# Feed-forward of a two-layer encoder: one weight group's casts held behind the last bank reads, and a spare tile for two of the seven down products

## The chip, the cores and the metric

The kernel runs on one core of a Trainium2 chip. The metric is the device time of one execution in microseconds (us). The core has a matrix engine (PE in the profile; PEld is its weight load), a vector engine (DVE), a scalar engine (ACT), a slower elementwise engine (POOL) and a sync engine (SP), whose queue issues nearly all transfers between HBM and the on-chip memory (SPq are its issues). Matrix products accumulate in eight banks, and DVE or ACT read them out. About 0.2% of the time (4.2 us) is the smallest difference that a measurement of this kernel tells from no change.

## The reference, cut to what matters

Two layers over 1024 tokens of width 1024. Each layer has a token mixer, a cross-attention to 256 memory tokens, an output projection, and then the feed-forward that this change touches:

```python
h = rmsnorm(x, norm_ffn[i])
gu = h @ w_gate_up[i]                                  # 1024 -> 2 * 2816
x = x + (jax.nn.silu(gu[..., :D_FF]) * gu[..., D_FF:]) @ w_down[i]   # 2816 -> 1024
```

All data are float32. After the second layer a final norm gives the output.

## The kernel before

Every product is made with operands that are split in two: `hi` (line 106, an ACT cast to the matrix engine's type) gives the rounded value, and `lo` (line 109, a DVE subtraction; its instruction stands at line 110 in the profile) gives the rest. Each product then takes three matmuls (high by high, high by low, low by high). A tile named `wd` holds the split weights of the down projection, a tile `hB` the split right operand.

The feed-forward multiplies by a seven-product scheme in place of eight products of half blocks (a Strassen form with few sums). It has two stages.

**Gate and up.** Units `Pair` (lines 1043 and on) make pairs of 128 output rows; 22 pairs, taken two at a time. For each two pairs the seventh products are made together by a unit `Fourth`, in three steps A, B and C. The matmuls of `Pair.product` stand at line 1101, those of `Fourth.part` at line 1183. A method `read` takes each finished bank out: ACT copies at lines 1112 to 1126 (the copy of product 4's bank X into `c` is line 1126), DVE additions through the helper at line 1109, and DVE subtractions through the helper at line 1211. The last steps of the stage, counted backwards as `to_go`, are: -6 the second pair's product 3, -5 step A, -4 its product 4, -3 step B, -2 its product 5, -1 step C. In step A bank Y is written in its low half, and `sub(a.c1[:, low], Y[:, low])` reads it; step B writes the high half of the same bank.

**Down.** Eleven row blocks are done as six groups `g` of two (the last has one). The products are numbered `i` in the code and go in the order 0, 1, 3, 2, 4, 5, 6; each has 132 matmuls (line 1532), 24 for a group of two. Products 0, 2 and 4 sum up in the four banks X, products 1 and then 3 and 5 in the four banks Y. After a product's last group `read(i, ...)` (the addition at line 1496) takes the banks out; product 3 begins Y anew, so it must wait for the reads of product 1, and product 4 goes on in X, so it waits for the reads of product 2.

`left_side(i, g)` (line 1406) makes the left operand of product `i`, group `g`. Raw weights come by transfer into a ring of five tiles `wd_raw` (`raw_tile`, 512 KB each) or into six tiles `wd_kept`. Product 0 uses a half `a` of `wd_kept`; product 3 loads two raw tiles and adds them into the other half `b` (line 1429); product 2 uses `b - a` (line 1423); product 4 loads two raw tiles and subtracts one from the other (line 1435); product 5 loads one and subtracts (line 1439). The result is cast into a ring of three tiles `wd`. `right_side(i, g)` reloads the right operand from HBM (`b_raw`) and casts it into `hB`.

`left_side` is called two groups ahead of use. For product 0 the calls stand inside the gate and up stage, by the table `ahead`: `left_side` of group 0 at `to_go` -5, of group 1 at -3. A scheduler in the framework sets the final order of each engine's queue: it takes instructions by priority as it expects their operands to be ready, so that the order is not the order of the code. Every queue is then run strictly in that order.

Of the kernel before, what the change touches and what calls it, by code (L numbers as in the profile page):

```python
# [41 lines left out]
def trunk_kernel(ctx: ExitStack, tc: tile.TileContext, a: dict, out: bass.AP):  # L42
# [59 lines left out]
    def raw_tile(name):  # L102

        return phase[0].tile([P, D], F32, tag="raw", name=name, bufs=phase[2])

    def hi(dst, src):
        nc.scalar.copy(dst, src)  # L107

    def lo(dst, src, h, eng=None):
        (eng or nc.vector).tensor_tensor(dst, src, h.bitcast(F32), op=ALU.subtract)  # L110

    def load_w(src, tag="whl", bufs=3, eng=None, name="w", pool=wp, parts=1, raw=None):
        if raw is None:
# [72 lines left out]
    class Norm:  # L186
# [82 lines left out]
        def raw(self, which):  # L269

            bc = self.scale()
            for k in range(NK):
                nc.vector.scalar_tensor_tensor(
                    self.xs[k], self.xs[k], gains[:, which, k : k + 1], bc, op0=ALU.mult, op1=ALU.mult
                )
                yield k
# [265 lines left out]
    for layer in range(2):  # L542
# [467 lines left out]
        with (  # L1010
# [32 lines left out]
            class Pair:  # L1043
# [62 lines left out]
                def read(self, n):  # L1106
                    self.seen.add(n)
                    X, Y = self.X, getattr(self, "Y", None)
                    add = lambda o, p_, q_, op=ALU.add: nc.vector.tensor_tensor(o, p_, q_, op=op)
                    if n == 0:  # L1110
                        self.g1 = temp("g1")
                        nc.scalar.copy(self.g1, X)
                    elif n == 1:
                        add(self.g1, Y, self.g1)
                        nc.scalar.activation(self.g1, self.g1, AF.Silu)
                    elif n == 2:
                        self.g2 = temp("g2")
                        nc.scalar.copy(self.g2, X)
                    elif n == 3:
                        self.c2 = temp("c2")  # L1120
                        nc.scalar.copy(self.c2, Y)  # L1121
                        if 4 in self.seen:
                            add(self.c2, self.c2, self.c1)
                    elif n == 4:
                        self.c1 = temp("c1")
                        nc.scalar.copy(self.c1, X)
                        if 3 in self.seen:
                            add(self.c2, self.c2, self.c1)
                        if 5 in self.seen:
                            add(self.c2, self.c2, self.g2, ALU.mult)  # L1130
                    elif n == 5:
                        add(self.g2, Y, self.g2)
                        nc.scalar.activation(self.g2, self.g2, AF.Silu)
                        if 4 in self.seen:
                            add(self.c2, self.c2, self.g2, ALU.mult)
                    else:
                        add(self.c1, self.c1, X, ALU.subtract)
                        add(self.c1, self.c1, self.g1, ALU.mult)
# [3 lines left out]
            class Fourth:  # L1142
# [65 lines left out]
                def read(self, n):  # L1208
                    (a, b), X, Y = self.units, self.X, self.Y
                    low, high = slice(0, h2), slice(h2, HS)  # L1210
                    sub = lambda c, ps, op=ALU.subtract: nc.vector.tensor_tensor(c, c, ps, op=op)
                    if n == "A":
                        sub(a.c1[:, low], X[:, low])
                        sub(a.c1[:, low], Y[:, low])
                    elif n == "B":
                        sub(a.c1[:, high], X[:, low])
                        sub(b.c1[:, high], Y[:, high])
                    else:
                        sub(
                            b.c1.rearrange("p (n c) -> p n c", n=2),  # L1220
                            X[:, low].unsqueeze(1).to_broadcast([P, 2, h2]),
                        )
                        sub(b.c1[:, low], X[:, high], ALU.add)
                        sub(b.c1, b.g1, ALU.mult)
                        sub(a.c1[:, high], Y[:, high])
                        sub(a.c1, a.g1, ALU.mult)
# [166 lines left out]
            def two(t, n):  # L1393
                return t.rearrange("p (n c) -> p n c", c=HS)[:, :n]
# [5 lines left out]
            def keep_rows(g):  # L1400
                if g not in kept:
                    p, n = groups[g]
                    kept[g] = fp.tile([P, 2, 2, HS], F32, tag="t8", name="wd_kept", bufs=6)[:, :n]
                    rows(kept[g][:, :, 0], g, 0, slice(0, HS))

            def left_side(i, g):

                p, n = groups[g]
                first_cols, second_cols = slice(0, HS), slice(HS, D)

                def raw():
                    return raw_tile("wd_raw").rearrange("p (n c) -> p n c", c=HS)[:, :n]

                if i == 0:
                    keep_rows(g)
                a, b = kept[g][:, :, 0], kept[g][:, :, 1]
                if i == 0:
                    src = a
                elif i == 1:
                    src = raw()  # L1420
                    rows(src, g, 1, first_cols)
                elif i == 2:
                    nc.vector.tensor_tensor(a, b, a, op=ALU.subtract)
                    src = a
                elif i == 3:
                    r, o = raw(), raw()
                    rows(r, g, 0, second_cols)
                    rows(o, g, 1, second_cols)
                    nc.vector.tensor_tensor(b, r, o, op=ALU.add)
                    src = b  # L1430
                elif i == 4:
                    src, o = raw(), raw()
                    rows(src, g, 0, first_cols)
                    rows(o, g, 0, second_cols)
                    nc.vector.tensor_tensor(src, src, o, op=ALU.subtract)
                elif i == 5:
                    src = raw()
                    rows(src, g, 1, first_cols)
                    nc.vector.tensor_tensor(src, src, a, op=ALU.subtract)
                else:  # L1440
                    src = raw()
                    rows(src, g, 1, second_cols)
                w = wp.tile([P, 2, D], F32R, tag="whl", name="wd", bufs=3)
                hi(two(w[:, 0], n), src)
                lo(two(w[:, 1], n), src, two(w[:, 0], n))
                for q in range(n):
                    left[i, p + q] = w[:, :, q * HS : (q + 1) * HS]

# [145 lines left out]
            }  # L1594
            for to_go in gate_up():
                for what, g in ahead.get(to_go, ()):
                    what(g) if what is keep_rows else what(0, g)
            norms = [Norm(row=None if is_a else next(factor_rows)), Norm()]
            ends = {c: Norm(HS // 2, 7) for c in quarter}
            dorder = [(i, g) for i in (0, 1, 3, 2, 4, 5, 6) for g in range(len(groups))]  # L1600
# [136 lines left out]
```

## Time and profile before

| what | value |
|---|---|
| three runs | 2115.09, 2116.83, 2116.86 us (median 2116.83) |
| the profiled execution's own time | 2115.94 us |
| its span, first to last instruction | 2114.2 us (so 1.74 us lie around it) |
| mean granted PE clock | 0.998 |
| PE, DVE, ACT, POOL busy | 99%, 72%, 51%, 28% of the span |
| HBM traffic | 133 GB/s over the span |

The first layer's feed-forward passes from gate and up to down at 814.45 us, the second layer's at 1888.38 us. A row of the timeline gives the start, the length from the first start to the last end of a merged run of equal instructions, engine, line, operation, output and inputs, shapes, count, and in square brackets the engine's idle time before it and what ended that. The end of a matmul is modelled by the profile; its start is recorded.

### The profile page before, as it was taken

What the parts mean: (1) busy time and instruction counts of PE and PEld (TensorE: products, weight loads), DVE (VectorE), ACT (ScalarE), POOL (GpSimd) and SP (SyncE); (2) the same over time, 40 slices, a digit from 0 to 9 for tenths busy, and PEclk for the clock granted to TensorE, in tenths of its full rate; (3) what the DMA queues carried; (4) which work ended last, traced back from release to release, by engine and by line L of the source; (5) the groups of instructions that cost most, each with busy time, mean ns of one, the idle gap of its engine ahead of it and who ended that gap; (6) DMA issues with size and microseconds to landing.
All of it is one profiled execution on the core that took longest, in us unless ns stands there. A gap on an engine that the chain in (4) does not pass through costs nothing.

```text
span 2114.2 us, 29053 instructions
## 1 busy us (share of the span) xinstructions
PE 2092.7 (99%) x10318; PEld 1750.1 (83%) x10318; DVE 1524.6 (72%) x2474; ACT 1077.9 (51%) x2037; POOL 583.6 (28%) x615
## 2 busy tenths in 40 slices
PE   9999999999999999999999999999999999999998
PEld 8788888888888888888888888888888888888887
DVE  7687886987666667776766666677986666677675
ACT  6687775544434335344466666664543434344443
POOL 0344330334444430000233223203243444400001
PEclk9999999999999999999999999999999999999999
DMA  6421128332333227866232222275232333267662
GB/s 232 146 82 51 36 83 288 99 115 100 110 108 111 91 105 254 313 216 207 78 110 68 69 72 78 64 266 157 75 110 105 110 115 104 91 254 256 205 221 95
DMA packets 121778, 288.08 MB, mean 136 GB/s; under 512 B 12705, under 2 KB 21153, under 8 KB 121633
## 3 DMA queue, kind: packets, MB, share of 16 engines
q1 hardware_dynamic: 113744, 272.42, 38.4%
q10 hardware_dynamic: 7888, 13.79, 1.7%
q8 instruction: 82, 1.34, 0.3%
q14 instruction: 64, 0.52, 0.1%
HBM read 211.19 MB, written 68.95 MB: 133 GB/s over the span
## 4 chain that ended last, share of the span: by engine, by line
PE 80%; issue 12%; DVE 3%; ACT 2%; POOL 2%; DMA 1%; POOLq 0%; ACTq 0%; SPq 0%; DVEq 0%
PE X L1101 16%; PE Y L1101 16%; PE mm L141 15%; PE po L141 8%; PE X L1532 5%; PE Y L1532 4%; PE O L809 3%; PE S L746 3%; PE pT L789 3%; PE X L1183 2%; PE Y L1183 2%; PE mm L448 1%; ACT p L761 1%; POOL wS L1058 1%; POOL wf L110 1%
## 5 line engine op out<-in xcount | busy, mean ns | idle before, releaser
L1101 PE MATMUL Y<-hB,wgu 128*128 128x512 f32 x1056 | 255.5, 391 | 0.8 <-ACT c L1121 0.8
L1101 PE MATMUL X<-hB,wgu 128*128 128x512 f32 x1056 | 254.8, 391 | 0.0
L1532 PE MATMUL X<-hB,wd 128*128 128x512 f32 (+1 forms) x1092 | 243.2, 383 | 0.9 <-DVE x L1496 0.9
L110 DVE TENSOR_TENSOR wgu<-wS,wgu 128x1024 fp32r<-128x1024 f32 (+1 forms) x124 | 155.4, 1253 | 120.9 <-ACT wgu L107 120.7
L1532 PEld LDWEIGHTS X<-hB,wd 128*128 128x128 f32 x1092 | 200.2, 188 | 41.4 <-issue 1.7
L1101 PEld LDWEIGHTS Y<-hB,wgu 128*128 128x128 f32 x1056 | 196.8, 188 | 43.4 <-ACT c L1121 1.6
L1101 PEld LDWEIGHTS X<-hB,wgu 128*128 128x128 f32 x1056 | 196.0, 188 | 39.8
L774 POOL TENSOR_SCALAR p<-p,stat 128x384 f32<-128x384 f32 (+1 forms) x256 | 143.1, 579 | 308.7 <-DVE stat L771 213.4
L141 PE MATMUL mm<-hT,wqk 128*128 128x512 f32 x672 | 199.3, 405 | 0.0
L107 ACT CAST wgu<-wS 128x1024 fp32r<-128x1024 f32 (+1 forms) x124 | 114.3, 923 | 142.0 <-POOL wS L1058 124.6
L141 PE MATMUL po<-yT,wo 128*128 128x512 f32 x768 | 184.2, 393 | 0.0
L1532 PE MATMUL Y<-hB,wd 128*128 128x512 f32 x792 | 180.4, 389 | 0.0
L1532 PEld LDWEIGHTS Y<-hB,wd 128*128 128x128 f32 x792 | 148.6, 188 | 31.2 <-DVE x L1496 0.4
L244 POOL TENSOR_TENSOR nr<-nv,neg_half 128x4 f32<-128x4 f32 (+1 forms) x12 | 13.3, 1105 | 582.9 <-DVE nv L243 573.7
L141 PEld LDWEIGHTS po<-yT,wo 128*128 128x128 f32 x768 | 142.7, 188 | 28.8 <-DVE yT L110 0.2
L1101 PE MATMUL X<-hT,wgu 128*128 128x512 f32 x624 | 150.2, 391 | 0.0
L107 ACT CAST hB<-b_raw 128x512 fp32r<-128x512 f32 x154 | 89.4, 618 | 115.5 <-DMA b_raw<-b_d 100.3
L1058 POOL TENSOR_TENSOR wS<-wgu_raw 128x512 f32<-128x512 f32 x44 | 61.2, 1391 | 292.1 <-DVE wgu L110 292.1
L1101 PEld LDWEIGHTS X<-hT,wgu 128*128 128x128 f32 x624 | 116.8, 188 | 26.3
L761 ACT ACTIVATE p<-p,stat 128x256 f32<-128x256 f32 (+1 forms) x192 | 112.4, 587 | 48.1 <-DVE stat L757 46.0
L110 DVE TENSOR_TENSOR pl<-pT,ph 128x384 fp32r<-128x384 f32 (+1 forms) x256 | 119.0, 493 | 19.1 <-ACT ph L107 15.9
L110 DVE TENSOR_TENSOR hB<-b_raw,hB 128x512 fp32r<-128x512 f32 x154 | 99.9, 687 | 42.2 <-ACT hB L107 42.1
(201 smaller groups left out, 4248.1 us busy)
## 6 DMA issues: line engine op xcount, KB each, us to landing
wgu_raw<-in_w_gu SPq DMA_DIRECT2D x92, 512.0 KB, 3.7
wd_raw<-in_w_dn SPq DMA_DIRECT2D x70, 512.0 KB, 4.4
b_raw<-b_d SPq DMA_DIRECT2D x70, 512.0 KB, 5.4
b_d<-c SPq DMA_DIRECT2D x88, 256.0 KB, 2.1
b_d<-t SPq DMA_DIRECT2D x66, 256.0 KB, 2.2
wo_raw<-in_w_out SPq DMA_DIRECT2D x32, 512.0 KB, 3.5
xr_d<-x ACTq DMA_DIRECT2D x32, 256.0 KB, 2.5
xr<-xr_d SPq DMA_DIRECT2D x16, 512.0 KB, 6.1
```

The costliest lines, as they stand in the source:

```text
L107: nc.scalar.copy(dst, src)
L110: (eng or nc.vector).tensor_tensor(dst, src, h.bitcast(F32), op=ALU.subtract)
L141: nc.tensor.matmul(ps[:, :n], l, r, start=start and i == 0 and j == 0, stop=stop and i == len(order) - 1 and j == 2,)
L746: nc.tensor.matmul(s_[:, :n], Q[self.h][:, qb * P : (qb + 1) * P], k, start=j == 0, stop=j == 1)
L761: nc.scalar.activation(p[:, :n], p[:, :n], AF.Exp, bias=m1, scale=-1.0, accum_out=s1)
L774: nc.gpsimd.tensor_scalar(p[:, :n], p[:, :n], ri[:, i : i + 1], 1.0, op0=ALU.mult, op1=ALU.mult)
L789: nc.tensor.transpose(tr[:, j * P : (j + 1) * P], p[:, j * P : (j + 1) * P], ident)
L809: nc.tensor.matmul(o[:, c0 : c0 + w * P], self.value(j), t[:, s0 : s0 + w].rearrange("p j q -> p (j q)"), start=j == js[0] and t is self.p ...
L1058: sub = lambda o, p_, q_: nc.gpsimd.tensor_tensor(o, p_, q_, op=ALU.subtract)
L1101: nc.tensor.matmul(ps, l, r, start=n in (0, 1, 3, 6) and k == 0 and i == 0, stop=k == 3 and i == 2, skip_group_check=True,)
L1183: nc.tensor.matmul(bank[:, at : at + h2], l, r, start=start and k == 0 and i == 0, stop=stop and k == 1 and i == 2, skip_group_check=True,)
L1532: nc.tensor.matmul(bank[:, c], l, r, start=i in (0, 1, 3, 6) and p == 0 and n == 0, stop=p == HF - 1 and n == 2, skip_group_check=True,)
```

## The change

First, `read` keeps two instructions of the last two pairs: the ACT copy of bank X of product 4 (`copied`) and the DVE subtraction that reads bank Y in step B (`summed`). The casts of `left_side(0, 1)`, group 1 of the down projection's product 0, get an ordering edge: the `hi` cast stands behind `copied` on ACT and the `lo` subtraction behind `summed` on DVE. The edge orders the queue of one engine and adds no semaphore wait.

Second, after the gate and up stage a tile `wd_other` of 128 x 2 x 1024 is taken from the pool slot `w8`, which the stage used for a weight tile (`wgu2`). Its two halves, by the parity of `g`, take the second raw operand of products 3 and 4, which used to come from the ring of five `wd_raw`. (In the short title of the change these are the fourth and fifth by number.)

```diff
-                        nc.scalar.copy(self.c1, X)
+                        self.copied = nc.scalar.copy(self.c1, X)
...
-                        sub(b.c1[:, high], Y[:, high])
+                        b.summed = sub(b.c1[:, high], Y[:, high])
...
-            def left_side(i, g):
+            def left_side(i, g, behind=()):
...
+                def other():
+                    t = spare[g % 2].bitcast(F32)
+                    return t.rearrange("p (n c) -> p n c", c=HS)[:, :n]
...
                 elif i == 3:
-                    r, o = raw(), raw()
+                    r, o = raw(), other()
...
                 elif i == 4:
-                    src, o = raw(), raw()
+                    src, o = raw(), other()
...
-                hi(two(w[:, 0], n), src)
-                lo(two(w[:, 1], n), src, two(w[:, 0], n))
+                with ExitStack() as queued:
+                    for ins in behind:
+                        queued.enter_context(tc.issue_after(ins.ins))
+                    hi(two(w[:, 0], n), src)
+                    lo(two(w[:, 1], n), src, two(w[:, 0], n))
...
-                    what(g) if what is keep_rows else what(0, g)
+                    if what is keep_rows:
+                        keep_rows(g)
+                    elif what is left_side:
+                        left_side(0, g, (us[-1].copied, us[-1].summed) if g == 1 else ())
+                    else:
+                        what(0, g)
+            spare = fp.tile([P, 2, D], F32R, tag="w8", name="wd_other", bufs=1)
+            spare = spare[:, 0], spare[:, 1]
```

The queues of PE and POOL keep their order. No instruction is added or left out on any engine; DVE, ACT and SP change their order in the stretch from step A to the end of the down projection, in both layers alike but for a few rows. Three places show it; the first layer's rows stand for both.

The first place is the end of gate and up on DVE. `wd<-wd_kept,wd` are the `lo` subtractions of the down groups, `c<-c,X` and `c<-c,Y` the reads of the banks of steps A and B. Before (-) and now (+):

```order
 L110 TENSOR_TENSOR wd<-wd_kept,wd 128x1024
 L1211 TENSOR_TENSOR c_7626<-c_7626,X_7746 128x256
-L110 TENSOR_TENSOR wd<-wd_kept,wd 128x1024
 L1211 TENSOR_TENSOR c_7626<-c_7626,Y_7747 128x256
 L1109 TENSOR_TENSOR c_7742<-c_7742,c_7777 128x512
 L1211 TENSOR_TENSOR c_7626<-c_7626,X_7746 128x256
 L1211 TENSOR_TENSOR c_7777<-c_7777,Y_7747 128x256
+L110 TENSOR_TENSOR wd<-wd_kept,wd 128x1024
```

Group 1's subtraction has moved from ahead of the read of bank Y to behind all four reads of steps A and B.

The second place is DVE ahead of the reads of product 1 (`x<-Y`), which free the banks Y for product 3. Before:

```order
L1429 TENSOR_TENSOR wd_kept<-wd_raw 128x2x512
L110 TENSOR_TENSOR wd<-wd_kept,wd 128x1024
L110 TENSOR_TENSOR hB<-b_raw,hB 128x512 x2
L1423 TENSOR_TENSOR wd_kept<-wd_kept 128x2x512
L1429 TENSOR_TENSOR wd_kept<-wd_raw 128x2x512
L1496 TENSOR_TENSOR x_01_8057<-Y,x_01_8057 128x512
L110 TENSOR_TENSOR wd<-wd_kept,wd 128x1024
```

Now, with the addition at line 1433, the subtraction `b - a` at line 1427 and the read at line 1503:

```order
L1433 TENSOR_TENSOR wd_kept<-wd_raw,wd_other 128x2x512
L110 TENSOR_TENSOR wd<-wd_kept,wd 128x1024
L110 TENSOR_TENSOR hB<-b_raw,hB 128x512 x2
L1433 TENSOR_TENSOR wd_kept<-wd_raw,wd_other 128x512
L1427 TENSOR_TENSOR wd_kept<-wd_kept 128x2x512
L1427 TENSOR_TENSOR wd_kept<-wd_kept 128x512
L1503 TENSOR_TENSOR x_01_8058<-Y,x_01_8058 128x512
L110 TENSOR_TENSOR wd<-wd_kept,wd 128x1024
```

The last addition of product 3 (the 128x512 one) and the last two subtractions of product 2 have moved ahead of the read; they stood behind it.

The third place is DVE ahead of the reads of product 2 (`x<-X`), which free the banks X for product 4. Before:

```order
L110 TENSOR_TENSOR wd<-wd_raw,wd 128x1024
L110 TENSOR_TENSOR hB<-b_raw,hB 128x512 x2
L1435 TENSOR_TENSOR wd_raw<-wd_raw 128x1024
L110 TENSOR_TENSOR wd<-wd_raw,wd 128x1024
L1496 TENSOR_TENSOR x_00_8736<-X,xr 128x512
L1496 TENSOR_TENSOR x_10_8741<-X,xr 128x512
```

Now:

```order
L110 TENSOR_TENSOR wd<-wd_raw,wd 128x1024
L110 TENSOR_TENSOR hB<-b_raw,hB 128x512 x2
L1503 TENSOR_TENSOR x_00_8729<-X,xr 128x512
L110 TENSOR_TENSOR wd<-wd_raw,wd 128x1024
L1503 TENSOR_TENSOR x_10_8734<-X,xr 128x512
```

Product 4's fifth subtraction (`wd_raw<-wd_raw` of 128x1024) has left the place ahead of the read; it now stands before the reads of product 3. In the second layer it stood behind these reads already, and there the sixth one (128x512) has come to stand directly ahead of the first `x<-X`.

On SP the first two `wd_other` transfers now go out behind the first reload `b_raw` of product 1, ahead of the other five.

More of the change, by code (lines that the diff above doesn't have):

```diff
@@ L106, in hi @@
     def hi(dst, src):
-        nc.scalar.copy(dst, src)
+        return nc.scalar.copy(dst, src)
     def lo(dst, src, h, eng=None):
-        (eng or nc.vector).tensor_tensor(dst, src, h.bitcast(F32), op=ALU.subtract)
+        return (eng or nc.vector).tensor_tensor(dst, src, h.bitcast(F32), op=ALU.subtract)
     def load_w(src, tag="whl", bufs=3, eng=None, name="w", pool=wp, parts=1, raw=None):
```

## The prediction

> **What bounds the kernel now.** I read the page's busy shares, then what PE waits for, then the timeline of PE through the two feed-forward stages, then DVE, ACT and SP at the places where PE stopped.
>
> ```profile
> span 2114.2 us, 29053 instructions
> PE 2092.7 (99%) x10318; PEld 1750.1 (83%) x10318; DVE 1524.6 (72%) x2474; ACT 1077.9 (51%) x2037; POOL 583.6 (28%) x615
> PE bc L266 <- DVE diag L252: 1.8, 2, 1.6
> PE Y L1183 <- DVE c L1211: 1.5, 1, 1.5
> PE X L1532 <- DVE x L1496: 0.9, 1, 0.9
> ```
>
> PE is busy 2092.7 of 2114.2 us, and its work is not changed. So the change can only win back time in which PE stands still. The waits list two such places inside the touched stretch, one each in line 1183 (gate and up) and line 1532 (down), 1.5 and 0.9 us. The other large one, 1.6 us of line 266, is in the kernel's tail. This caps the gain near 3 us, or 0.14%: less than the 0.2% that a measurement can tell. What is open is whether the new order of DVE makes other stops.
>
> **Term 1: the last steps of gate and up.** Second layer's PE rows, then the first layer's:
>
> ```profile
> 1880.27 0.88 PE L1183 MATMUL X<-q4h,wgu 128*128 128x256 f32 x6
> 1882.67 0.97 PE L1183 MATMUL Y<-hT,wgu 128*128 128x256 f32 x6 [1.53 <-DVE c L1211]
> 1883.48 2.90 PE L1101 MATMUL Y<-hB,wgu 128*128 128x512 f32 x12
> 1886.22 1.60 PE L1183 MATMUL X<-q4h,wgu 128*128 128x256 f32 x12
> 1887.66 0.88 PE L1183 MATMUL Y<-hT,wgu 128*128 128x256 f32 x6
> ...
> 808.04 0.88 PE L1183 MATMUL X<-q4h,wgu 128*128 128x256 f32 x6
> 809.54 2.91 PE L1101 MATMUL Y<-hB,wgu 128*128 128x512 f32 x12
> ```
>
> Twelve matmuls of this form take 1887.66 - 1886.22 = 1.44 us from start to start. Step B's twelve took 1883.48 - 1880.27 = 3.21 us in the second layer and 809.54 - 808.04 = 1.50 in the first, so 1.77 and 0.06 us were lost. Why, is on ACT and DVE:
>
> ```profile
> 1879.98 1.05 ACT L107 CAST wd<-wd_kept 128x1024 fp32r<-128x1024 f32 x1 [1.37 <-DMA wd_kept<-in_w_dn]
> 1880.93 0.58 ACT L1126 COPY c<-X 128x512 f32<-128x512 f32 x1
> 1879.30 0.41 DVE L1211 TENSOR_TENSOR c<-c,X 128x256 f32<-128x256 f32 x1
> 1881.06 1.23 DVE L110 TENSOR_TENSOR wd<-wd_kept,wd 128x1024 fp32r<-128x1024 f32 x1 [1.35 <-ACT wd L107]
> 1882.20 0.41 DVE L1211 TENSOR_TENSOR c<-c,Y 128x256 f32<-128x256 f32 x1
> ```
>
> Group 1's cast waited on ACT for its transfer, its subtraction waited on DVE for the cast, and the read of bank Y stood behind it; PE got the bank at 1882.61 and went on at 1882.67. With the subtraction behind the four reads, the read of Y runs at about 1879.7, right after that of X, and PE starts Y at 1880.27 + 0.72 = 1880.99, before any of this. What is late next? The ACT copy no longer stands behind the cast: it waits only for PE's bank, whose last matmul starts just before 1880.27, and ends near 1881.0. The DVE reads of step B end near 1882.4, well before step C (now from about 1884.5). The moved cast then runs at 1881.0 to 1882.1 and the subtraction to about 1883.6. Its user, the down stage's group 1, starts 24 matmuls (5.4 us) into the down stage, at 1888.4 - 1.8 + 5.4 = 1892.0, so 8 us cover the move. The same holds in the first layer. Gain: 1.77 + 0.06 = 1.83 us.
>
> **Term 2: the start of product 4.** PE, then DVE and the issue that the chain comes from:
>
> ```profile
> 814.45 30.11 PE L1532 MATMUL X<-hB,wd 128*128 128x512 f32 x132
> 844.39 60.00 PE L1532 MATMUL Y<-hB,wd 128*128 128x512 f32 x264
> 904.23 30.08 PE L1532 MATMUL X<-hB,wd 128*128 128x512 f32 x132
> 935.18 30.21 PE L1532 MATMUL X<-hB,wd 128*128 128x512 f32 x132 [0.87 <-DVE x L1496]
> 965.23 30.08 PE L1532 MATMUL Y<-hB,wd 128*128 128x512 f32 x132
> ...
> 928.52 0.38 SPq L1398 DMA_DIRECT2D wd_raw<-in_w_dn  x1
> 932.08 1.22 DVE L1435 TENSOR_TENSOR wd_raw<-wd_raw 128x1024 f32<-128x1024 f32 x1 [2.38 <-DMA wd_raw<-in_w_dn]
> 933.22 1.22 DVE L110 TENSOR_TENSOR wd<-wd_raw,wd 128x1024 fp32r<-128x1024 f32 x1
> 934.35 2.48 DVE L1496 TENSOR_TENSOR x<-X,xr 128x512 f32<-128x512 f32 x4
> ```
>
> An unhindered product takes 844.39 - 814.45 = 29.94 us. Product 2 to the start of product 4 took 30.95, product 4 itself 30.05: 1.01 + 0.11 = 1.12 us lost. A raw tile came free at 928.5, its transfer landed at 932.1, and the subtraction and a `lo` stood ahead of the read of X. With the second operand in its own tile this transfer needs no slot so late, and the subtraction now stands some 30 us earlier in the queue. The read can run at about 932.4, when PE leaves the first bank. In the second layer there was no stop here, and now a 128x512 subtraction stands ahead of the read:
>
> ```profile
> 2002.71 0.38 SPq L1398 DMA_DIRECT2D wd_raw<-in_w_dn  x1
> 2006.50 0.69 DVE L1496 TENSOR_TENSOR x<-X,xr 128x512 f32<-128x512 f32 x1 [0.50 <-PE X L1532]
> wd_raw<-in_w_dn SPq DMA_DIRECT2D x7, 256.0 KB, 5.5
> ```
>
> Its raw tile comes free when the `lo` of product 4's group 0 ends, which is when SP issued a raw transfer before (2002.71). PE needs the bank at 2008.3 (before's clock), so with 0.6 for the subtraction and 0.69 for the read the transfer may take 4.3 us. The first layer's median for 256 KB was 5.5 us under load (the last row), which would cost 1.2 us; but here only one reload is in flight. Bounds 0 and 1.2; I take 0.
>
> Gain of the two terms: 1.83 + 1.12 = 2.95 us. By the idle times alone it would be 1.53 + 0.87 = 2.40; I go by the starts, since the profile models a matmul's end. [...]
>
> **Term 3: the reads of product 1, where DVE gets more to do first.** This is the place that can take the gain back.
>
> ```profile
> 822.00:845.00 23.00, 23.00 (x103) 19.07 (x102) 12.40 (x17) 11.15 (x17) 0.00 (x0) 1.00 0.53 182
> 845.00:873.00 28.00, 28.00 (x126) 23.17 (x125) 23.93 (x28) 10.58 (x16) 0.00 (x0) 1.00 0.95 352
> DVE wd_kept L1429 <- DMA wd_raw<-in_w_dn: 1.9, 2, 1.3
> DVE hB L110 <- ACT hB L107: 1.2, 2, 0.9
> DVE wd L110 <- ACT wd L107: 0.9, 2, 0.7
> 872.86 0.68 DVE L1496 TENSOR_TENSOR x<-Y,x 128x512 f32<-128x512 f32 x1
> 874.59 1.88 DVE L1496 TENSOR_TENSOR x<-Y,x 128x512 f32<-128x512 f32 x3
> 1918.32 60.26 PE L1532 MATMUL Y<-hB,wd 128*128 128x512 f32 x264
> 1947.25 0.69 DVE L1496 TENSOR_TENSOR x<-Y,x 128x512 f32<-128x512 f32 x1
> ```
>
> The second row is the 28 us up to these reads in the first layer: DVE busy 23.93 (its third figure), DMA engines busy 0.95 at 352 GB/s; the row above it is the stretch before, with 0.53 and 182; the next three are DVE's waits in the second row's window, 4.0 us in all. PE needs the first bank at 844.39 + 29.92 = 874.31 and the second 1.36 us later, at 875.67. The second read ended at 874.59 + 0.68 = 875.27, so the first may start 0.40 us later than it did, at 873.26, for nothing. In the second layer the need is at 1918.32 + 29.92 = 1948.24 and 1.36 us later, and the read's start at 1947.25 was at that edge.
>
> The new order puts ahead of the read: an addition (128x512, 0.60), two subtractions (1.14 and 0.60) and one more pair of `hB` (1.20): 3.54 us. DVE would reach the read at 845 + 23.93 - 0.14 + 3.54 = 872.3 without any wait, so 0.9 of the 4.0 us of waits may stay. If all stay, each layer loses 3.1 us; if none, nothing, and the second layer may gain a quarter of a microsecond. I take the lower end, 0.2 us a layer, because the waits have a reason that goes: two of the transfers (1.05 MB, 3.0 us at 352 GB/s) no longer wait for raw tiles and go out soon after 822, when the engines were half idle, and the third, fourth and fifth raw tiles come free as soon as an addition ends. The additions then fill the gaps in which DVE waited for `hB`.
>
> What else moves costs nothing as long as its cover holds. Two transfers stand ahead of five reloads of product 1: those come about 3 us later. The shortest lead of an `hB` in the first layer's down stage is that of product 2's fifth group: made from 911.13, used from 904.23 + 4 x 5.44 = 925.99, so 14 us cover it (a group of 24 matmuls takes 29.94 x 24 / 132 = 5.44 us). `wd_other` holds two groups, so on SP a transfer waits for the subtraction two groups back, with reloads queued behind it; two groups last 10.9 us of PE, and a raw transfer took at most 8.5 us in this stage:
>
> ```profile
> 911.13 1.29 DVE L110 TENSOR_TENSOR hB<-b_raw,hB 128x512 fp32r<-128x512 f32 x2
> DMA to landing us min/median/max: 2.5/5.3/8.5
> ```
>
> The slot `w8` was last read in the gate and up stage's product 3, before the down stage, so its first transfers wait for nothing. Sum: -1.83 - 1.12 + 0.4 = -2.55 us, against the profiled execution's 2115.94: 2113.4. That execution is 0.89 us under the median of the three runs, by which it would be 2114.3. I forecast 2113.6.
>
> **The rivals.** (A) *The waits of term 3 stay and become PE stops; slower.* It decides at 0.9 + 2.95 / 2 = 2.4 us of DVE waits left in each layer: from there on the kernel is slower. For it: the DMA engines are at 0.95 in that window, and the order now needs 0.5 MB more by then. Against: 1.05 MB left it. With all 4.0 us kept: -2.95 + 6.2 = +3.3, 2119.2; with half of that, 2116.1. [...]
>
> (B) *Term 2 only moves.* Other raw transfers still wait for slots, and the read of X stays behind a late one, now in the second layer: 1.12 not won, 1.2 lost. 2113.4 + 1.1 to + 2.3 = 2114.5 to 2115.7. For it: the new 128x512 subtraction ahead of that read. Against: the 4.3 us allowed there.
>
> (C) *The change does not do what it says*: the edges or the tile leave the waits where they are. The order of DVE shows the read of Y ahead of the subtraction, so nearly excluded for term 1; 2115.9.
>
> (D) *More than 4 us faster.* PE's idle time elsewhere would have to fall; none of it waits for what is moved.
>
> **How the numbers follow.** Forecast (both stops gone, term 3 under 0.7 us a layer): 0.66. (A) with a loss: 0.17, of it 0.05 over +4.2 us, if new waits join the old ones. (B) 0.12. (C) 0.03. (D) 0.02. Range: 2111.5 (no loss, the low run of 2115.09 less 2.95, and 0.6 for chip and run) to 2117.2 (half of A at the median's level, 2116.1 + 0.9, and 0.2). Faster by over 0.2%: (D) and a low draw of the forecast, 0.04; slower: 0.05; within 0.2%: 0.91.
>
> **What would show it.** Right: no PE wait for `c L1211` after step B's X, twelve matmuls of step B in 1.44 us in both layers; product 2 to 4 in 29.94; the first `x<-Y` of product 1 starting by 873.3 in the first layer's old time. Wrong: PE idle at the start of product 3 with DVE's `x` named, a `wd_raw` or `wd_other` transfer as the releaser of line 1433; or PE idle at the second layer's product 4 behind line 1439.

## The result, and the profile after

| | kernel before | changed kernel |
|---|---|---|
| time, median of 22 runs each | 2117.56 us (2114.70 to 2119.66) | 2113.82 us (2112.57 to 2117.04) |
| ratio, 95% interval | | 0.9983 (0.9977 to 0.9989) |
| profiled execution: time, span | 2115.94, 2114.2 us | 2114.71, 2112.7 us |

The change saves 0.17%, or 3.7 us of the medians (2.3 to 4.9 by the interval). The interval does not reach 1, so over this many runs a difference smaller than the 4.2 us named ahead can be told from no change. The forecast was 2113.6 us. Three executions in the comparisons below ran at a granted clock of 0.65 to 0.86 over the whole and took 140 us and more longer; no median here counts them.

The profiled executions differ by less, 1.5 us of span, and each engine has as many instructions as before. The busy time on the page after, and PE's wait in line 223 after and before (us in total, times, longest):

```profile
PE 2093.2 (99%) x10318; PEld 1750.9 (83%) x10318; DVE 1523.9 (72%) x2474; ACT 1078.2 (51%) x2037; POOL 585.0 (28%) x615
PE st L223 <- DVE sq L230: 1.5, 3, 0.8
PE st L223 <- DVE sq L230: 0.8, 1, 0.8
```

The two waits that the prediction named, for `c` of line 1211 and for `x` of the down projection's read, are no longer in the list of PE's waits. This execution won 2.9 us back at the places that the change touches, as shown next, but lost 0.8 us to four matmuls at its end, which took 1.93 us against 1.10 (last section), and about 0.6 us elsewhere outside these places; its waits in line 223 are 0.7 us longer. PE's timeline through the two feed-forward stages shows where the time came back (start, us, then the instruction; line 1539 is the down product, 1532 before):

```profile
805.38 2.94 PE L1101 MATMUL X<-hB,wgu 128*128 128x512 f32 x12
814.80 30.11 PE L1539 MATMUL X<-hB,wd 128*128 128x512 f32 x132
844.75 60.00 PE L1539 MATMUL Y<-hB,wd 128*128 128x512 f32 x264
904.59 60.00 PE L1539 MATMUL X<-hB,wd 128*128 128x512 f32 x264
964.42 30.08 PE L1539 MATMUL Y<-hB,wd 128*128 128x512 f32 x132
...
1877.28 2.91 PE L1101 MATMUL X<-hB,wgu 128*128 128x512 f32 x12
1886.37 3.81 PE L1539 MATMUL X<-hB,wd 128*128 128x512 f32 x16
1916.32 60.00 PE L1539 MATMUL Y<-hB,wd 128*128 128x512 f32 x264
1976.16 60.00 PE L1539 MATMUL X<-hB,wd 128*128 128x512 f32 x264
2036.00 4.24 PE L1539 MATMUL Y<-hB,wd 128*128 128x512 f32 x18
```

Three distances between starts measure all that the change can touch. The first, "end", runs from the 12 matmuls `X<-hB,wgu` ahead of step B to the first down product: 9.09 us when nothing waits (1886.37 - 1877.28). The other two, "P3" and "P4", run over two down products each, up to product 2 and up to product 5: 59.84 us when nothing waits. What exceeds these is lost to stops. Here P3 and P4 are 59.84 in both layers (59.83 once), the second layer's end is 9.09, and the first layer's is 9.42 with 0.33 lost. Before, 3.26 us were lost: 1.84 at the end, 0.26 at P3, 1.16 at P4. The rows of before that this takes beside those shown ahead:

```profile
805.29 2.91 PE L1101 MATMUL X<-hB,wgu 128*128 128x512 f32 x12
1877.52 2.91 PE L1101 MATMUL X<-hB,wgu 128*128 128x512 f32 x12
1978.42 60.00 PE L1532 MATMUL X<-hB,wd 128*128 128x512 f32 x264
```

DVE and ACT in the second layer, at the place where PE stood for 1.53 us before:

```profile
1879.33 0.41 DVE L1211 TENSOR_TENSOR c<-c,X 128x256 f32<-128x256 f32 x1
1879.85 0.42 DVE L1211 TENSOR_TENSOR c<-c,Y 128x256 f32<-128x256 f32 x1
1882.12 1.22 DVE L110 TENSOR_TENSOR wd<-wd_kept,wd 128x1024 fp32r<-128x1024 f32 x1
1880.23 0.59 ACT L1126 COPY c<-X 128x512 f32<-128x512 f32 x1 [1.59 <-PE X L1101]
1880.71 1.05 ACT L107 CAST wd<-wd_kept 128x1024 fp32r<-128x1024 f32 x1
```

The read of Y follows that of X at once, and the cast and the subtraction come when the banks are free. The prediction had put the read at 1879.7 and the subtraction's end at 1883.6; they came at 1879.85 and 1883.3, in an execution that is 0.24 us earlier at this place (1877.28 and 1877.52).

In the first layer, the window of the prediction ahead of product 1's reads (DVE's busy time is its third figure):

```profile
845.00:873.00 28.00, 28.00 (x125) 23.21 (x124) 27.24 (x34) 11.56 (x17) 0.00 (x0) 1.00 0.94 346
```

DVE does 3.31 us more there than before (23.93). Its only wait in this window, and the reads behind it:

```profile
DVE hB L110 <- ACT hB L107: 0.7, 1, 0.7
```

```profile
872.98 0.69 DVE L1503 TENSOR_TENSOR x<-Y,x 128x512 f32<-128x512 f32 x1
874.71 1.89 DVE L1503 TENSOR_TENSOR x<-Y,x 128x512 f32<-128x512 f32 x3
```

It waits 0.7 instead of 4.0 us, and none of it for a transfer of weights. The transfers into the spare tile are no faster than the others, as the page's list of DMA issues shows (number, size, median us to landing):

```profile
wd_raw<-in_w_dn SPq DMA_DIRECT2D x50, 512.0 KB, 4.0
wd_other<-in_w_dn SPq DMA_DIRECT2D x20, 512.0 KB, 7.2
```

They are issued early enough for their 7.2 us to be hidden: the first two went out from 822.97 on, for additions that start at 849.38 and 852.92.

### The profile page after: what moved, and what is told of

Same layout as the page of the kernel before. It is cut to its first block, busy times and chain, and to the rows that moved or that the text cites. A ratio compares the mean times of both kernels' runs of the same rounds, so it can differ in the third digit from the quotient of the medians.

```text
span 2112.7 us, 29026 instructions
## 1 busy us (share of the span) xinstructions
PE 2093.2 (99%) x10318; PEld 1750.9 (83%) x10318; DVE 1523.9 (72%) x2474; ACT 1078.2 (51%) x2037; POOL 585.0 (28%) x615
## 3 DMA queue, kind: packets, MB, share of 16 engines
q8 instruction: 82, 1.34, 0.3%
## 4 chain that ended last, share of the span: by engine, by line
PE 80%; issue 12%; DVE 3%; ACT 2%; POOL 2%; DMA 0%; POOLq 0%; ACTq 0%; DVEq 0%
PE X L1101 16%; PE Y L1101 16%; PE mm L141 15%; PE po L141 8%; PE X L1539 5%; PE Y L1539 4%; PE O L809 3%; PE S L746 3%; PE pT L789 3%; PE X L1183 2%; PE Y L1183 2%; PE mm L448 1%; ACT p L761 1%; POOL wS L1058 1%; POOL wf L110 1%
```

## The experiments

Each kernel's loss is read from its one profiled execution by the three distances above, both layers added; its time is the median of its runs, beside the difference to the runs of the kernel before on the same chip (with the 95% interval of the ratio, in us).

| kernel | end | P3 | P4 | lost | median us | against before |
|---|---|---|---|---|---|---|
| changed kernel | 0.33 | 0 | 0 | 0.33 | 2113.82 | -3.7 (-4.9 to -2.3) |
| the same, second profile | 0 | 0 | 0 | 0 | 2112.44, one run | |
| both groups held | 0 | 0 | 0 | 0 | 2114.08 | -3.5 (-5.7 to -1.9) |
| tile in product 3 only | 0.54 | 0 | 0.52 | 1.06 | 2114.61 | -2.8 (-4.9 to -1.1) |
| DVE's edge alone | 0 | 0.41 | 1.19 | 1.60 | 2115.43 | -1.9 (-3.8 to 0) |
| tile in product 4 only | 0 | 1.77 | 0 | 1.77 | 2115.45 | -1.9 (-4.4 to -0.4) |
| end read nine times | 2.18 | 0 | 0 | 2.18 | 2116.07 | -1.3 (-3.2 to 0.8) |
| edges alone | 0 | 1.17 | 1.36 | 2.53 | 2116.45 | -1.1 (-3.0 to 0.8) |
| one half of the tile | 0 | 1.46 | 0.42 | 1.88 | 2116.47 | -0.9 (-3.2 to 0.8) |
| tile alone | 4.62 | 0 | 0 | 4.62 | 2116.67 | -0.9 (-3.0 to 0.8) |
| four more subtractions | 0 | 2.81 | 1.13 | 3.94 | 2117.36 | -0.2 (-1.7 to 2.1) |
| kernel before, first profile | 1.84 | 0.26 | 1.16 | 3.26 | 2117.35 to 2117.56 | |
| kernel before, second profile | 2.27 | 0.57 | 1.25 | 4.09 | 2117.25, one run | |
| end read seven times | 2.48 | 1.57 | 1.10 | 5.15 | 2118.05 | 0.7 (-1.3 to 3.0) |

The medians rise with the lost time, from 2113.8 to 2114.1 at none or 0.33 to 2116.7 and more at 3.3 to 5.2: to within about 1 us the stops at these three places account for what the kernels differ by. The tile alone is nearly 2 us off, and its profiled execution was the slowest of its eleven (2121.62 us). No single pair of neighbours in the list is told apart by its times.

**The edges alone.**

```diff
-                    r, o = raw(), other()
+                    r, o = raw(), raw()
...
-                    src, o = raw(), other()
+                    src, o = raw(), raw()
...
-            spare = fp.tile([P, 2, D], F32R, tag="w8", name="wd_other", bufs=1)
-            spare = spare[:, 0], spare[:, 1]
```

> The two edges alone; both operands of products 3 and 4 in raw tiles as before. Theory (the two terms are independent): step B's twelve matmuls start 1.44 us apart from step B to step C in the second layer instead of 3.21; product 2 to product 4 in the first layer still takes 30.5 to 31.1 us, with PE's wait for DVE's x at its end; DVE waits 3 to 4 us in the 28 us ahead of product 1's reads. Time 1.5 to 2.1 us under the kernel before. Rival (the stop at step B only moves to step C, because the four reads still wait for the late ACT copy): step B and C together as long as before, time within 0.5 us of before. Rival (the spare tile carries the whole gain): no change.

The end lost nothing in either layer, so the stop did not move to step C, and product 4 stood as before (1.36 us). The gain was 1.1 us, less than expected, and P3 lost 1.17 us. DVE's wait there in the first layer, and then PE's row and DVE's:

```profile
DVE wd_kept L1433 <- DMA wd_raw<-in_w_dn: 3.1, 3, 1.8
```

```profile
845.69 60.54 PE L1539 MATMUL Y<-hB,wd 128*128 128x512 f32 x264
874.91 0.68 DVE L1503 TENSOR_TENSOR x<-Y,x 128x512 f32<-128x512 f32 x1
```

The read starts 874.91 - 845.69 = 29.22 us after product 1's first matmul; before it was 872.86 - 844.39 = 28.47, after 872.98 - 844.75 = 28.23, with three microseconds more of work ahead. Left to raw tiles, the additions wait for transfers, and how long differs from profile to profile: in the first layer DVE waited 1.9 us for them ahead of these reads before, 3.1 here and 3.5 with the tile in product 4 only.

**The tile alone.**

```diff
-                        left_side(0, g, (us[-1].copied, us[-1].summed) if g == 1 else ())
+                        left_side(0, g)
```

> The spare tile alone, no edges. Theory: step B in the second layer still takes 3.0 to 3.3 us with PE's wait for DVE's c of line 1211; product 2 to product 4 takes 29.9 to 30.0 us in the first layer; DVE waits under 1 us ahead of product 1's reads, product 1 to product 3 in 59.84 us for both products. Time 1.0 to 1.5 us under the kernel before. Together with the run of the edges alone the gains add up to 2.9 us, what the two traces differ by. Rival (one gain needs the other): the sum of the two runs is under 2 us.

P3 and P4 lost nothing; the end lost 4.62 us. The gains of the two kernels add up to 2.0 us and not to 3.7, which is where the rival stood (under 2), but with intervals of near 2 us on either side this decides nothing. By place each half does its part without the other: the edges alone clear the end, the tile alone P3 and P4. In this execution the stop at step B had a sequel. PE's rows, and then the window behind the stop (the third figure from the end is the granted clock):

```profile
1885.76 0.98 PE L1183 MATMUL Y<-hT,wgu 128*128 128x256 f32 x6 [1.80 <-DVE c L1211]
1886.58 4.50 PE L1101 MATMUL Y<-hB,wgu 128*128 128x512 f32 x12
1890.92 1.60 PE L1183 MATMUL X<-q4h,wgu 128*128 128x256 f32 x12
```

```profile
1887.10:1890.50 3.40, 3.40 (x10) 2.66 (x9) 1.39 (x3) 1.04 (x2) 0.00 (x0) 0.50 0.65 245
```

The twelve matmuls of product 5 took 1890.92 - 1886.58 = 4.34 us, against 1886.22 - 1883.48 = 2.74 in the kernel before, with the clock at 0.50 for 3.4 us: behind the stop of 1.80 us another 1.60 us were lost.

**DVE's edge alone, without the tile** (`(us[-1].summed,)` in place of both, the rest as with the edges alone).

> DVE's edge alone, without ACT's and without the spare tile: group 1's subtraction stands behind the four reads, its cast ahead of the copy of bank X on ACT as in the kernel before. Theory (only DVE's order mattered, the copy is covered): step B's twelve matmuls in 1.44 us in both layers, step C starts at once, though the copy waits for the cast; product 2 to product 4 in 30.5 to 31.2 in the first layer; time as with both edges alone, 2116.5, within 0.7 us. Rival (the copy behind the late cast holds the sum c+c, and with it the reads of step B): step C starts 0.5 to 1.5 us late in the second layer, time 0.5 to 1.5 us above that of both edges.

ACT's rows in the second layer:

```profile
1879.61 1.05 ACT L107 CAST wd<-wd_kept 128x1024 fp32r<-128x1024 f32 x1 [0.47 <-DMA wd_kept<-in_w_dn]
1880.88 0.59 ACT L1126 COPY c<-X 128x512 f32<-128x512 f32 x1 [0.21 <-PE X L1101]
```

The cast went ahead of the copy, the end lost nothing, and product 4's stop stayed. But the copy waited for PE, not for the cast: the cast came 1.68 us after the start of the twelve matmuls (1877.93) and before it had come 2.46 us after it (1879.98 and 1877.52). So DVE's edge is enough where the transfer is no later than this; a later one, which would hold the copy, was not seen, and the rival stays untested for that case. The time is 1.0 us under that of both edges, a little more than the 0.7 allowed, and the intervals overlap.

**Both groups held**: group 0's left side is made after step B and gets the same two edges as group 1's.

```diff
-                        left_side(0, g, (us[-1].copied, us[-1].summed) if g == 1 else ())
+                        left_side(0, g, (us[-1].copied, us[-1].summed))
...
-                -5: [(left_side, 0)],
...
-                -3: [(left_side, 1)],
+                -3: [(left_side, 0), (left_side, 1)],
```

> The change, and group 0's cast and subtraction held behind the same two reads as group 1's. Theory: in the first layer step A's 12 matmuls to step B's start and on to product 5 take 4.25 us or less (the changed kernel 4.51, the kernel before 4.25), because no subtraction stands ahead of the read of bank X; the second layer's steps are as in the changed kernel; nothing waits at the start of the down projection, since group 0's subtraction ends near 1883.3 and is used from 1886.5. Time 0.2 to 0.4 us under the changed kernel, 3.0 to 4.1 under the kernel before. Rival (two subtractions behind each other delay the down projection): PE waits in the down projection's first products for DVE's wd or hB, 0.5 to 2 us a layer, and the gain is lost.

PE's rows at the two ends of the first layer's stretch:

```profile
805.28 2.91 PE L1101 MATMUL X<-hB,wgu 128*128 128x512 f32 x12
814.38 30.11 PE L1539 MATMUL X<-hB,wd 128*128 128x512 f32 x132
```

The first layer's end is 9.10 us, with the 0.33 of the changed kernel gone, and nothing waits later. The times (2114.08 and 2113.82) can't tell a third of a microsecond, and the changed kernel itself lost nothing here in its second profile. It is no slower, and the only version in which no subtraction stands ahead of these reads.

**The tile in product 4 only, and in product 3 only.** In the first, `r, o = raw(), raw()` in product 3; in the second, `src, o = raw(), raw()` in product 4.

> The change, but product 3's second operand stays in a raw tile; only product 4 uses the spare one. Theory (product 3's tile is what takes DVE's waits for transfers away ahead of product 1's reads): DVE waits 2 to 4 us there for wd_raw as with the edges alone, products 1 and 3 together take 60.2 to 60.5 us in both layers instead of 59.84; product 2 to product 4 in 29.9 to 30.4 (a 128x512 subtraction stands ahead of the read of X); time 0.7 to 1.5 us above the changed kernel, 2.2 to 3.0 under the kernel before. Rival (the stops at product 3 with the edges alone were chance): 59.84 in both layers, time as the changed kernel.

> The change, but product 4's second operand stays in a raw tile; only product 3 uses the spare one. Theory of the prediction's second term (product 4's own slot is what comes late): a raw transfer of product 4 is issued within 8 us of the read of X and PE stops 0.5 to 1.1 us at product 4 in the first layer; time 0.5 to 1.1 us above the changed kernel. Rival (the ring of raw tiles was behind since product 3, which alone relieves it; in this order the late subtractions stand behind the reads): products 1 and 3 in 59.84, product 2 to product 4 in 29.94, time as the changed kernel within 0.5 us.

DVE's wait for raw transfers ahead of product 1's reads, and PE, with the tile in product 4 only:

```profile
DVE wd_kept L1433 <- DMA wd_raw<-in_w_dn: 3.5, 3, 2.1
```

```profile
874.59 30.50 PE L1539 MATMUL Y<-hB,wd 128*128 128x512 f32 x132 [0.79 <-DVE x L1503]
```

P3 loses 1.37 and 0.40 us, the first more than expected. So it is product 3's use of the tile that clears these reads. With the tile in product 3 only, P3 loses nothing (the 0.54 at its end lie behind group 0's subtraction, which ends as the read of X starts, in both layers) and P4 0.52, at the lower end of what the second term's theory said, and its raw transfer went out at 927.28, 4.9 us ahead of the read. But what stood ahead of the read on DVE was not its subtraction:

```profile
930.98 1.29 DVE L110 TENSOR_TENSOR hB<-b_raw,hB 128x512 fp32r<-128x512 f32 x2 [0.69 <-ACT hB L107]
932.19 0.69 DVE L1503 TENSOR_TENSOR x<-X,xr 128x512 f32<-128x512 f32 x1
```

The scheduler left one `hB` more ahead of the read than in the changed kernel, and the pair waited for ACT. How much of the 0.52 comes from the raw slot and how much from this order stays open.

**One half of the tile for all groups** (`t = spare[0].bitcast(F32)`).

> The change, with one half of the spare tile for all groups instead of two in turn, so that each of its transfers waits for the subtraction or addition of the group just before, not of two groups back. Theory (a group takes 5.44 us of PE; a transfer of 512 KB took 5.3 us by the median and up to 8.5, and an addition 1.2, so one half is not enough and two are): DVE waits 2 to 6 us for wd_other ahead of product 1's reads, PE stops 0.5 to 3 us a layer at product 3 or in the groups after it; time 1 to 5 us above the changed kernel. Rival (the transfers have enough lead with one half): no PE stop over 0.3 us in products 1 to 5, time as the changed kernel.

DVE's wait in the second layer's last 30 us ahead of product 1's reads, and PE's stop behind them:

```profile
DVE wd_kept L1433 <- DMA wd_other<-in_w_dn: 2.6, 4, 1.2
```

```profile
1946.89 30.50 PE L1539 MATMUL Y<-hB,wd 128*128 128x512 f32 x132 [0.86 <-DVE x L1503]
```

DVE waits for the tile's transfers again (1.5 us in the first layer, 2.6 in the second), P3 loses 0.02 and 1.44 us, and the time is 2.6 us above the changed kernel. One half is not enough and two are, as the prediction's step on the cover said.

**Four more subtractions ahead of product 1's reads.**

```diff
-                    nc.vector.tensor_tensor(a, b, a, op=ALU.subtract)
+                    for _ in range(5 if g == 0 else 1):
+                        nc.vector.tensor_tensor(a, b, a, op=ALU.subtract)
```

> The change, with group 0's subtraction of product 2 done five times instead of once (its value is the same but for rounding): four more 128x1024 subtractions, 1.14 us each, in each layer. Two of them and one more lo (1.14) stand ahead of product 1's first read, and one of 0.60 behind it instead: 2.82 us more of DVE work there. Theory (after the change DVE has no idle time left ahead of these reads, and they may start about 0.7 us later for nothing): PE stops at the start of product 3 for 1.5 to 2.2 us in the first layer, with DVE's x named; 1.2 to 2.2 in the second; time 2.7 to 4.4 us above the changed kernel, that is within 1.5 us of the kernel before. Rival (DVE still has idle time there, as in the kernel before): no stop, time as the changed kernel, 3 to 4 us under the kernel before.

PE's rows at the start of product 3 in the two layers:

```profile
875.36 30.18 PE L1540 MATMUL Y<-hB,wd 128*128 128x512 f32 x132 [1.47 <-DVE x L1504]
1948.72 30.20 PE L1540 MATMUL Y<-hB,wd 128*128 128x512 f32 x132 [0.81 <-DVE x L1504]
```

P3 loses 1.73 and 1.08 us (the second a little under what was expected), P4 another 1.13, and the time is 3.5 us above the changed kernel. Of the 2.82 us added, 1.73 and 1.08 came back as stops, so DVE has less than 1.8 us left ahead of these reads: the slower rival of the prediction is real, and 2.8 us of DVE work bring it about.

**Both kernels profiled again.**

> The kernel before, unchanged, profiled once more on another occasion. Theory (the stops hang on when single transfers land, so their sizes change from execution to execution while their places stay): PE stops in steps A and B of both layers together 0.8 to 3.0 us (1.83 in the first profile), at the start of product 3 in both layers together 0.3 to 1.8 us (0.26 in the first profile, 0.41 to 1.77 in the kernels whose product 3 takes raw tiles), at product 4 of the first layer 1.0 to 1.3. Rival (the stops are fixed by the order of the queues): the sizes of the first profile within 0.1 us at each of the three places.

> The changed kernel, profiled once more. Theory: no stop over 0.1 us at product 3 or 4 in either layer (59.84 us for each pair of products); in steps A and B 0 to 0.4 us a layer, where group 0's subtraction stands ahead of the read of bank X. Rival (it was a lucky execution): stops of 0.4 us and more at product 3 or 4.

The second profile of the kernel before, ACT in the second layer and then PE's stops:

```profile
1880.25 1.05 ACT L107 CAST wd<-wd_kept 128x1024 fp32r<-128x1024 f32 x1 [1.45 <-DMA wd_kept<-in_w_dn]
808.64 0.98 PE L1183 MATMUL Y<-hT,wgu 128*128 128x256 f32 x6 [0.22 <-DVE c L1211]
1882.94 0.98 PE L1183 MATMUL Y<-hT,wgu 128*128 128x256 f32 x6 [1.53 <-DVE c L1211]
935.48 30.19 PE L1532 MATMUL X<-hB,wd 128*128 128x512 f32 x132 [0.99 <-DVE x L1496]
```

The three places are the same and the sizes vary: 4.09 us lost instead of 3.26, most of the difference at the first layer's end (0.48 for 0.07) and at P3. The second layer's stop at step B was the same to 0.01. The changed kernel lost nothing the second time. These are single runs; one more run of the kernel before beside them took 2120.17 us.

**A longer stop at step B, to see its sequel.** The read of Y in the last step A is done seven times, or nine times, over:

```diff
                         sub(a.c1[:, low], Y[:, low])
+                        for _ in range(3 if b is us[-1] else 0):
+                            sub(a.c1[:, low], Y[:, low], ALU.add)
+                            sub(a.c1[:, low], Y[:, low])
```

> The change, with the read of bank Y in the last step A of each layer done seven times over (subtracted, then added and subtracted three times more; the value is the same but for rounding). The last of them ends about 2.0 us after PE wants the bank: PE stops about 2.0 us at step B in each layer, like the stop of 1.80 us in the kernel with the tile alone, after which the granted clock fell to 0.50 to 0.70 and 12 matmuls took 4.34 us instead of 2.75. [...] Rival (the slow stretch was a disturbance that has nothing to do with the stop): granted clock 1.00 after both stops, time 4.0 us above the changed kernel.

> As the kernel with the stop of 2 us, but the read is done nine times over, and the last of them stands behind an hB subtraction that waits for its transfer: PE stops 3 to 4.5 us at step B in each layer. [...]

PE's rows with the seven reads, second layer, and then the window behind the stop:

```profile
1882.30 1.54 PE L1101 MATMUL Y<-hB,wgu 128*128 128x512 f32 x6
1884.92 0.98 PE L1183 MATMUL Y<-hT,wgu 128*128 128x256 f32 x6 [1.08 <-DVE c L1211]
```

```profile
1884.90:1889.00 4.10, 4.08 (x28) 3.83 (x29) 3.14 (x6) 2.25 (x4) 0.00 (x0) 1.00 0.68 249
```

These two missed their aim. The scheduler put matmuls of product 5 ahead of step B's second half (first row), so that no stop at step B was longer than 1.08 us, where 2.0 and 3 to 4.5 were meant, and the clock stayed at 1.00 behind that one (last row). With seven reads the time was 4.2 us above the changed kernel, near the 4.0 named, but by other stops than the ones meant; with nine it was 2.3 above. So they say nothing of what follows a longer stop. They show by the way that a later read costs less when PE's order gives way too: with nine reads the loss at the end was no greater (2.18 us) than with seven (2.48).

The seven reads also changed DVE's order in the down projection, with both halves of the tile in use. In the first layer, ahead of the reads of product 1 and then of product 2:

```profile
873.38 1.22 DVE L110 TENSOR_TENSOR wd<-wd_kept,wd 128x1024 fp32r<-128x1024 f32 x1
874.51 2.48 DVE L1506 TENSOR_TENSOR x<-Y,x 128x512 f32<-128x512 f32 x4
934.55 0.69 DVE L1442 TENSOR_TENSOR wd_raw<-wd_raw,wd_other 128x512 f32<-128x512 f32 x1
935.16 0.69 DVE L1506 TENSOR_TENSOR x<-X,xr 128x512 f32<-128x512 f32 x1
```

One `lo` more stood ahead of the first reads, and P3 lost 0.90 and 0.67 us, though DVE waited for no transfer of weights there. A 128x512 subtraction behind a later `hB` stood ahead of the second, and P4 lost 1.10 us in the first layer. So the tile takes the waits for transfers away, and the order of the queue can still bring the stops back.

## Why the prediction was right, and where it was not

**What bounds the kernel.** PE was the bound, and the gain came from its stops and stayed under 0.2%, as said. The cap of near 3 us was too low: the medians moved by 3.7. It was read from the list of waits, which names 2.4 us of stops in the touched stretch; by the starts that same execution lost 3.26 us, and another of the same kernel 4.09.

**Term 1** was right for the second layer: 1.77 us forecast and gained, by the mechanism named; the stop was there in all three profiles without the edges (1.77 and 1.79 before, 2.12 at step B with the tile alone), and in none with them. The 0.06 us of the first layer failed. The step "the same holds in the first layer" left out that group 0's subtraction still stands ahead of the read of bank X (it ran from 806.75 to 807.98 us, the read from 807.89), and that layer lost 0.33 in the first profile after and nothing in the second. With both groups held it lost nothing.

**Term 2** had the right size: 1.12 us forecast, 1.16 found, 1.16 to 1.36 lost in the four profiles without the tile. The bound taken for the second layer, 0 of 0 to 1.2, was right (59.84 us). Its reason is shown in part only: the tile in product 4 alone brought P4 to 0, in product 3 alone to 0.52, and in that last case the read stood behind other work than the one named.

**Term 3** is the step that failed, by its sign. Its parts were near: 3.54 us more work forecast and 3.31 found, at most 0.9 us of waits to stay and 0.7 stayed, a start by 873.26 in the old time and 872.98 - 0.36 = 872.62 in it. The price put on them, a loss of 0.2 us a layer, was wrong: nothing was lost, and 0.26 us was won against the first profile, 0.57 against the second. The prediction had named a quarter of a microsecond in the second layer as possible and left it out of the sum. What it missed is that the raw tiles' order lost time at these reads already, and that its profile showed little of that by chance: the last 35 steps of DVE ahead of these reads are the same in the five profiles that feed product 3 from raw tiles, and P3 lost 0.26, 0.41, 0.57, 1.17 and 1.77 us in them. The four other kernels that fed product 3 from raw tiles or from one half lost 0.41 to 1.77 us at P3; with the tile's two halves nothing was lost in the five profiles in which DVE had no added work. With added work it was again: in two of the three kernels that had it (four more subtractions, seven reads) stops came back at P3.

**The sum.** -2.55 us forecast; -2.93 by the first profiles of both (3.26 - 0.33), -4.09 by the second, -3.7 by the medians. That the forecast hit 2113.82 so closely is luck, because a second error ran the other way: it was made against an execution of 2115.94, with 0.2 of the 0.89 us to the median of three runs added, and over 22 runs the median of before was 2117.56. The gain was some 1.2 us too small and the base some 1.4 too low.

**The rivals.** (A), the waits of term 3 stay: out, though the added subtractions show that its price is real. (B), term 2 only moves: out, 59.84 us in both layers; its price is real too, as the seven reads show (1.10 us at P4). (C): out, both stops went. (D), over 4 us: not reached by the median, though the interval ends at 4.9. The transfers into the spare tile took 7.2 us by the median over the kernel, the raw ones of 512 KB before 4.4; what took the waits away was the earlier issue.

## What to carry to other kernels

In an in-order queue a step that waits for a transfer belongs behind the reads that free PE's banks, as long as its user is far enough away; here 8 us of cover made a 1.8 us stop vanish. Where a ring of load tiles delays work ahead of such reads, a tile of its own for the second operand can pay for more work ahead of them (3.31 us of it here, with the waits down from 4.0 to 0.7 us). With transfers of 7.2 us and groups of 5.44 us it took two halves here; with one, P3 lost 1.46 us. And the order of the queue still decides what stands ahead of the reads. One profile shows where the stops are, not how large they are on average: two of the same kernel differed by 0.8 of 4 us, so a sum of terms of this size should be set against several.

## What the hardware showed beside this

In the tile-alone kernel the granted clock was 0.50 over 3.4 us (1887.10 to 1890.50) behind the stop of 1.80 us at step B, and the twelve matmuls of product 5 took 4.34 us there against 2.74 in the kernel before. The same execution has one more stretch at 0.50, behind a stop of 0.91 us and eight `st` matmuls:

```profile
400.11 1.05 PE L223 MATMUL st<-inv_d,sq 128*128 128x1 f32 x8 [0.91 <-DVE sq L230]
402.30:405.70 3.40, 3.40 (x9) 2.59 (x8) 0.69 (x1) 0.23 (x1) 0.17 (x1) 0.50 0.00 0
```

In the kernel before, the stop of 1.53 us at step B had no such sequel: in both profiles the clock was 1.00 over the 5 us behind it. What makes the difference was not shown.

At the kernel's end PE runs twelve `st` matmuls, stands 1.63 us in every one of the fourteen profiles, and runs four matmuls `bc`, which took 1.10 us in six of them and 1.34 to 2.05 us in the other eight:

```profile
2105.84 1.10 PE L266 MATMUL bc<-diag,ones 128*128 128x256 f32 x4 [1.63 <-DVE diag L252]
2106.21 2.04 PE L266 MATMUL bc<-diag,ones 128*128 128x256 f32 x4 [1.63 <-DVE diag L252]
```

These are the first and the second profile of the kernel before: the same stop, and 0.94 us between them. The granted clock was 0.96 in the first (2105.8 to 2107) and 0.50 in the second (2106 to 2108). The four matmuls took 1.93 us at 0.54 in the changed kernel's first profile (2103.5 to 2105.6) and 1.34 us at 0.72 with both groups held (2103.3 to 2105). So 0.94 of the 1.3 us by which the spans of the two profiles of before differ (2114.2 and 2115.5) comes from this place, which the change doesn't touch.
